# A DeltaNet layer whose decay comes from selecting products and a mask, whose triangular and attention matrices are written transposed, and whose projections and groups of heads run in another order

## The chip, the cores and the metric

One core of one Trainium2 chip runs the whole program. The metric is the device time of one execution in microseconds (us); smaller is better. The engines are TensorE (PE, its weight loads PEld), VectorE (DVE), ScalarE (ACT), GpSimd (POOL) and the queue of SyncE (SP), which issues nearly all DMAs. All data is float32; the program splits operands into a high and a low part and multiplies them in three products, so that the results keep float32 accuracy.

## The reference

256 tokens of width 1024 pass through two layers: a retention mixer and a gated DeltaNet mixer, each followed by a SwiGLU mixer of width 2816. The change is in DeltaNet alone:

```python
qkv = silu(causal_depthwise_conv(proj_qkv, conv_w))      # 8 q heads, 8 k heads, 16 v heads of 128
q, k = l2norm(q) * 128 ** -0.5, l2norm(k)                # each shared by two v heads
g = -exp(a_log) * softplus(a + dt_bias)                  # log decay per token and v head
gcum = cumsum(g)                                         # within a chunk
decay_mat = where(causal, exp(gcum[:, None] - gcum[None, :]), 0)
a_mat = where(strict, (k * beta) @ k.T * decay_mat, 0)
u, w = triangular_solve(a_mat + eye, [v * beta, k * beta * exp(gcum)])
attn = where(causal, q @ k.T * decay_mat, 0)
# per chunk, with the state S carried on:
v_new = u - w @ S
o = (q * exp(gcum)) @ S + attn @ v_new
S = S * exp(g_last) + (k * exp(g_last - gcum)).T @ v_new
o = rmsnorm(o) * silu(z);  out = o @ w_out
```

The kernel uses chunks of 128 tokens, so there are two (c = 0 and 1).

## The kernel before

**Weights.** Every weight matrix comes in slabs of 128x1024 numbers (`slab`, lines 124 to 137): a DMA from SP's queue into `raw`, a copy on ACT into `whi` (line 131), a subtraction on DVE into `wlo` (line 133), three buffers of each. A slab then feeds 12 matmuls of 512 columns (projections by token: z and the output) or 24 of 256 columns (projections by channel: k, q and v), all through `mm3`, lines 139 to 141. There are 260 slabs; 64 belong to DeltaNet: 16 for z, 8 for k, 8 for q, 16 for v and 16 for the output. q, k and v also pass a convolution of four taps: one on ACT (line 721) and three on DVE (line 724) for each block of 128 channels, and a SiLU on ACT.

**Order.** `gdn` lists jobs in the order z0, k, q, z1, v0, z2, v1, v2, v3, z3 (z and v in four groups of four heads), then the output projection. Beside the jobs run generators, one step after each slab: `gates` (decay), `sumsq_T` and `amat` (norms and the matrix A), `invert` (the inverse of I + A), `attn`, and `inner` for each group of four heads. A tile scheduler then orders each engine's instructions once and for all, when the program is built; at run time each engine works in order and waits for semaphores.

**Decay.** `gates` makes, for 8 sets of four heads, two tiles 128x512 (`gmh`, `gml`, line 691, on DVE and POOL), which line 714 multiplies by an upper triangle; ACT takes the exponential of 512 columns at a time (line 715). POOL sets what lies above the diagonal to zero (line 806).

**A and its inverse.** Line 768 makes k k.T, and A is that times beta and decay: on DVE for chunk 0 (line 778), on ACT and POOL for chunk 1 (lines 773, 774). The diagonal blocks of 32 go to DRAM and back in another layout (lines 797, 799); DVE inverts 128 of them side by side in 31 steps (lines 813, 815); the result goes through DRAM again (lines 820, 823: `Vd`, `Vc`). Then TensorE joins blocks to 64 (lines 849, 857, 864) and to 128 (lines 873, 882), chunk 0 before chunk 1, with an ACT copy after each step.

**Attention and heads.** Line 914 makes q k.T, ACT copies it, POOL multiplies it by the decay (`att`, line 917), TensorE transposes, ACT copies back into `D`. `inner` solves (line 938), moves the state (line 952), attends (line 946), takes norms (line 984, POOL's power in line 987), scales by z (line 995) and transposes for the output projection (`yh`, `yl`), which starts with group 0 and needs group 3 for its last quarter.

Of the kernel before, what the change touches and what calls it, by code (L numbers as in the profile page):

```python
# [61 lines left out]
class Trunk:  # L62
# [264 lines left out]
    def out_proj(self, w, yT, nk, nxt, early=None):  # L327
# [45 lines left out]
        p0 = self.proj_tok(w, 0, 512, yT, nk, None, (early,) if early else (), (), first)  # L373
        p1 = self.proj_tok(w, 512, 512, yT, nk, None, (early,) if early else (), (last,), second)
# [258 lines left out]
    def gates(self, b):  # L633
# [19 lines left out]
        nega, ax, e, u, ln, ru, g, gl = (tmp[:, i] for i in range(8))  # L653
# [26 lines left out]
        b["beta"] = beta  # L680

        slb = self.SL.unsqueeze(1).broadcast_to([P, 4, P])
        f4 = lambda x: x.rearrange("p h j -> p (h j)")
        b["D"] = [self.big(f"D{c}") for c in range(NT)]
        pend = []
        for c in range(NT):
            for hg in range(4):
                hs = slice(hg * 4, hg * 4 + 4)
                gm = [self.t2(n, dt=F32R) for n in ("gmh", "gml")]
                for eng, x, y in zip((V, V if hg % 2 else G), gm, (gh.bitcast(F32), gl)):  # L690
                    eng.tensor_tensor(x, slb, y[:, c, hs].unsqueeze(2).broadcast_to([P, 4, P]), ALU.mult)
                pend.append((c, hs, gm))
                if len(pend) == 3:
                    self.decay(b, Ur, *pend.pop(0))
                if hg % 2:
                    yield
                if c == 0 and hg == 1:

                    gs = self.psip()
                    for x in range(NT):  # L700
                        T.matmul(gs[:, x * NH:(x + 1) * NH], self.U, g[:, x], start=True, stop=True)
                    T.matmul(gs[:, 2 * NH:3 * NH], self.SL, g[:, 0], start=True, stop=True)
                    eg, dec = sm("eg"), sm("dec", (NH,))
                    A_.activation(eg.rearrange("p c h -> p (c h)"), gs[:, 0:2 * NH], AF.Exp)
                    A_.activation(dec, gs[:, 2 * NH:3 * NH], AF.Exp)
                    b["eg"], b["dec"] = eg, dec
        for x in pend:
            self.decay(b, Ur, *x)
        b["decayed"] = True

    def decay(self, b, Ur, c, hs, gm):
        dp = self.psip()
        for i, x in enumerate(gm):
            self.nc.tensor.matmul(dp, Ur, x.rearrange("p h j -> p (h j)"), start=i == 0, stop=i == 1)
        b["exp"] = self.nc.scalar.activation(b["D"][c][:, hs].rearrange("p h j -> p (h j)"), dp, AF.Exp).ins
# [30 lines left out]
    def amat(self, b, sl):  # L746


        nc = self.nc
        V, G, A_, T = nc.vector, nc.gpsimd, nc.scalar, nc.tensor  # L750
        yield
        ks, hs = slice(2 * sl, 2 * sl + 2), slice(4 * sl, 4 * sl + 4)
        rk = self.ph.tile([P, NT, 2], F32, name="rk", bufs=2)
        V.tensor_scalar(rk, b["kss"][:, :, ks], EPS, None, ALU.add)
        G.tensor_tensor(rk, rk, self.mhalf[:, 0:4].rearrange("p (t h) -> p t h", t=NT), ALU.pow)
        yield
        rkb = rk.unsqueeze(3).broadcast_to([P, NT, 2, 2])
        w2 = lambda x: x[:, :, hs].rearrange("p t (h w) -> p t h w", w=2)
        beta1, beta2 = b["beta1"], b["beta2"]
        V.tensor_tensor(w2(beta1), w2(b["beta"]), rkb, ALU.mult)  # L760
        V.tensor_tensor(w2(beta2), w2(beta1), rkb, ALU.mult)
        V.scalar_tensor_tensor(b["beg"][:, hs], beta2[:, 1, hs], -1.0, b["eg"][:, 1, hs], ALU.mult, ALU.mult)
# [20 lines left out]
    def invert(self, b):  # L783
# [19 lines left out]
        for c in range(NT):  # L803
            for hg in range(4):
                dm = b["D"][c][:, hg * 4:hg * 4 + 4]
                G.affine_select(dm, dm, [[0, 4], [-1, P]], ALU.is_ge, 0.0, base=0, channel_multiplier=1)
# [3 lines left out]
        for i in range(31):  # L810
# [3 lines left out]
                            Ab[:, n:32, i].unsqueeze(1).broadcast_to([P, n, m]), ALU.mult)  # L814
# [12 lines left out]
        yield  # L827
        yield
# [4 lines left out]
        V.transpose(Tc.rearrange("p a b -> p (a b)"), Vc.rearrange("p a b -> p (a b)"))  # L833
# [3 lines left out]
        for c in range(NT):  # L837
# [9 lines left out]
            for h in range(NH):  # L847
                for (q, b0, b1), x in zip(blocks, xp):
                    T.matmul(x[b0, h], Am[c][b1, h, b0], Vc[b1, c * NH + h], start=True, stop=True,
                             tile_position=(32 * q + 32, 32 * q))  # L850
            for (q, b0, b1), x in zip(blocks, xp):
                A_.copy(X[b0], x[b0])
            yield
            vp = [h32(self.psip()) for _ in blocks]
            for h in range(NH):
                for (q, b0, b1), x in zip(blocks, vp):
                    T.matmul(x[b0, h], Tc[b0, c * NH + h], X[b0, h], start=True, stop=True,
                             tile_position=(32 * q, 32 * q))
# [4 lines left out]
            for h in range(NH):  # L863
                T.matmul(tq[b1, h], X[b0, h], Tc[b0, c * NH + h], start=True, stop=True, tile_position=(0, 32))
# [4 lines left out]
            for hg in range(2):  # L869
                xp = h64(self.psip())  # L870
                for j in range(8):
                    h = hg * 8 + j
                    T.matmul(xp[lo, j], Am[c][up, h, lo], Vf[c][up, h, up], start=True, stop=True,
                             tile_position=(64, 0))
                X2.append(self.t2("X2", (8, 64), p=64))
                A_.copy(X2[hg], xp[lo])
            yield
            for hg in range(2):
                vp = h64(self.psip())
                for j in range(8):  # L880
                    h = hg * 8 + j
                    T.matmul(vp[lo, j], T2[lo, h], X2[hg][:, j], start=True, stop=True, tile_position=(0, 0))  # L882
# [4 lines left out]
    def attn(self, b):  # L887
# [13 lines left out]
        def flush(c, hp, at):  # L901
            tp = self.pstp().rearrange("p (x j) -> p x j", j=P)
            for j in range(4):
                self.transpose(tp[:, j], at[:, j])
            nc.scalar.copy(b["D"][c][:, 4 * hp:4 * hp + 4], tp)

        pend = None
        for c in range(NT):
            cs = slice(c * P, (c + 1) * P)
            for hp in range(4):  # L910
                at = self.t2("att")
# [283 lines left out]
```

## Time and profile before

| | us |
|---|---|
| median of 3 runs (873.5 to 874.11) | 873.65 |
| the profiled execution | 873.93 |
| its span, first to last instruction | 872.1 |
| DeltaNet in it, from its first weight-side matmul to the end of the output projection | 409.4 to 674.1 |

| in DeltaNet | us from the span's start |
|---|---|
| z0 | 409.4 to 419.7 |
| k, decay among it | 419.7 to 447.0 |
| q | 447.0 to 477.3 |
| z1 | 477.3 to 490.4 |
| v0, z2 | 490.4 to 524.7 |
| v1, v2, v3 | 524.7 to 577.4 |
| z3, the second chunk's inverse | 577.4 to 593.3 |
| the heads, no projection | 593.3 to 625.8 |
| output projection | 625.8 to 674.1 |

The page puts TensorE at 97% of the span, VectorE at 64%, ScalarE at 52% and GpSimd at 7%. The ends of matmuls are modelled, so what a matmul costs in a full stream is read from one start to the next. The granted clock is an average over a stretch of TensorE's two levels, 2.4 GHz (1.0) and 1.2 GHz (0.5).

### The profile page before, as it was taken

The numbers are of one execution on the slowest core, as the hardware profiler recorded it, in microseconds if no ns is written. First come the engines' busy times: TensorE is split into PE (matmuls) and PEld (weight loads), VectorE is DVE, ScalarE is ACT, GpSimd is POOL, SyncE is SP. The second block draws the span as 40 slices with busy tenths as digits, with TensorE's granted clock in tenths as the row PEclk, the third lists the DMA queues.
The fourth block names the chain that finished last, engine by engine and source line by source line (L and its number), as shares of the span: only waits on it lengthen the run. The fifth ranks groups of instructions, "written<-read, shape, count | busy, mean of one in ns | idle before, by whom it ended". The sixth has DMA issues, their size and how long they took to land.

```text
span 872.1 us, 12737 instructions
## 1 busy us (share of the span) xinstructions
PE 843.0 (97%) x4903; PEld 720.0 (83%) x4903; DVE 555.6 (64%) x828; ACT 453.0 (52%) x770; POOL 59.0 (7%) x59
## 2 busy tenths in 40 slices
PE   6999999999999999999999988999899999999996
PEld 5889987887788889886998878989788888889885
DVE  4957877655555555455889899854665555555453
ACT  5553235554544444344587745687845544444343
POOL 1000000000000000000217141000200000000000
PEclk9999999999999999999999999999999999999999
DMA  8666445455556555554555734732045656555551
GB/s 254 208 190 173 123 146 166 172 191 195 178 183 192 181 183 176 187 191 121 145 146 130 210 109 136 206 107 74 1 166 171 198 188 190 177 188 176 186 193 72
DMA packets 121806, 143.54 MB, mean 165 GB/s; under 512 B 14145, under 2 KB 67826, under 8 KB 121746
## 3 DMA queue, kind: packets, MB, share of 16 engines
q1 hardware_dynamic: 121234, 141.48, 51.7%
q0 software_dynamic: 368, 1.19, 0.5%
q8 instruction: 38, 0.62, 0.3%
q14 instruction: 22, 0.18, 0.1%
q10 hardware_dynamic: 144, 0.07, 0.0%
HBM read 140.62 MB, written 2.10 MB: 164 GB/s over the span
## 4 chain that ended last, share of the span: by engine, by line
PE 37%; DVE 8%; issue 2%; DMA 2%; ACT 2%; POOL 1%; SPq 0%; POOLq 0%; ACTq 0%; DVEq 0%
PE mm L140 10%; PE mm L141 10%; PE mm L139 10%; DVE wlo L133 2%; PE tp L200 1%; DVE cacc L724 1%; PE ip L952 1%; DVE pr L813 1%; DMA raw<-gdn_w_in 1%; PE ip L938 1%; PE ip L946 1%; DMA Vc<-Vd 1%; DMA Vd<-Vb 0%; DVE Vb L815 0%; PE ip L882 0%
## 5 line engine op out<-in xcount | busy, mean ns | idle before, releaser
L133 DVE TENSOR_TENSOR wlo<-raw,whi 128x1024 fp32r<-128x1024 f32 x260 | 321.0, 1235 | 231.5 <-ACT whi L131 229.5
L131 ACT CAST whi<-raw 128x1024 fp32r<-128x1024 f32 x260 | 273.4, 1052 | 300.3 <-PE mm L140 227.7
L139 PE MATMUL mm<-whi,xh 128*128 128x512 f32 (+1 forms) x576 | 220.5, 386 | 2.5 <-ACT whi L131 1.7
L140 PE MATMUL mm<-whi,xl 128*128 128x512 f32 (+1 forms) x576 | 219.8, 382 | 0.5 <-DVE xl L311 0.3
L141 PE MATMUL mm<-wlo,xh 128*128 128x512 f32 (+1 forms) x576 | 208.6, 383 | 1.2 <-DVE wlo L133 1.2
L139 PEld LDWEIGHTS mm<-whi,xh 128*128 128x128 f32 x576 | 109.3, 190 | 22.4 <-ACT whi L131 2.2
L141 PEld LDWEIGHTS mm<-wlo,xh 128*128 128x128 f32 x576 | 108.7, 189 | 21.9 <-DVE wlo L133 1.9
L140 PEld LDWEIGHTS mm<-whi,xl 128*128 128x128 f32 x576 | 109.0, 189 | 20.9 <-issue 0.7
L139 PE MATMUL mm<-xh,whi 128*128 128x256 f32 x384 | 111.9, 291 | 0.0
L140 PE MATMUL mm<-xh,wlo 128*128 128x256 f32 x384 | 110.2, 287 | 1.2 <-DVE wlo L133 1.2
L141 PE MATMUL mm<-xl,whi 128*128 128x256 f32 x384 | 109.8, 286 | 0.0
L140 PEld LDWEIGHTS mm<-xh,wlo 128*128 128x128 f32 x384 | 74.2, 193 | 3.3 <-DVE wlo L133 1.8
L139 PEld LDWEIGHTS mm<-xh,whi 128*128 128x128 f32 x384 | 74.1, 193 | 1.3 <-issue 0.5
L141 PEld LDWEIGHTS mm<-xl,whi 128*128 128x128 f32 x384 | 74.1, 193 | 0.3
L139 PE MATMUL mm<-whi,hh 128*128 128x512 f32 x176 | 69.8, 396 | 0.0
L140 PE MATMUL mm<-whi,hl 128*128 128x512 f32 x176 | 69.6, 396 | 0.0
L141 PE MATMUL mm<-wlo,hh 128*128 128x512 f32 x176 | 64.3, 396 | 0.0
L724 DVE SCALAR_TENSOR_TENSOR cacc<-mm,conv,cacc 128x253 f32<-128x253 f32 (+2 forms) x96 | 45.6, 511 | 9.0 <-ACT cacc L721 8.4
L140 PE MATMUL mm<-whi,yl 128*128 128x512 f32 x128 | 50.4, 394 | 0.0
L139 PE MATMUL mm<-whi,yh 128*128 128x512 f32 x128 | 49.5, 394 | 0.9 <-DVE v L995 0.9
L141 PE MATMUL mm<-wlo,yh 128*128 128x512 f32 x128 | 49.2, 396 | 0.0
L141 PEld LDWEIGHTS mm<-wlo,hh 128*128 128x128 f32 x176 | 33.1, 188 | 8.1
(235 smaller groups left out, 877.3 us busy)
## 6 DMA issues: line engine op xcount, KB each, us to landing
raw<-ffn_w_in SPq DMA_DIRECT2D x88, 512.0 KB, 3.5
raw<-ret_w_in SPq DMA_DIRECT2D x48, 512.0 KB, 3.9
raw<-gdn_w_in SPq DMA_DIRECT2D x48, 512.0 KB, 3.9
raw<-ffn_w_out SPq DMA_DIRECT2D x44, 512.0 KB, 3.5
raw<-ret_w_out SPq DMA_DIRECT2D x16, 512.0 KB, 3.2
raw<-gdn_w_out SPq DMA_DIRECT2D x16, 512.0 KB, 3.6
h<-x SPq DMA_DIRECT2D x4, 256.0 KB, 7.3
out<-o SPq DMA_DIRECT2D x4, 256.0 KB, 2.2
```

The lines of the kernel that those rows point to most:

```text
L131: nc.scalar.copy(hi, raw)
L133: lo_ = nc.vector.tensor_tensor(lo, raw, hi.bitcast(F32), ALU.subtract)
L139: t.matmul(out, lh, rh, start=first, stop=False)
L140: t.matmul(out, ll, rh, start=False, stop=False)
L141: self.last_mm = t.matmul(out, lh, rl, start=False, stop=last).ins
L200: self.nc.tensor.transpose(out, in_, self.ident[:n, :n])
L724: self.nc.vector.scalar_tensor_tensor(acc[:, s:S], ps[:, 0:S - s], cw[:, i, blk:blk + 1], acc[:, s:S], ALU.mult, ALU.add)
L813: V.tensor_tensor(tmp, Vb[:, 0:n, i:i + 1].broadcast_to([P, n, m]), Ab[:, n:32, i].unsqueeze(1).broadcast_to([P, n, m]), ALU.mult)
L938: T.matmul(up[:, j], b["V"][c][:, 4 * hg + j], v[c][:, j], start=True, stop=True)
L946: T.matmul(op[:, j], b["D"][c][:, 4 * hg + j], uu[:, j], start=True, stop=True)
L952: T.matmul(f4(op[:, 2 * j:2 * j + 2]), x(2 * hg + j), f4(st[:, 2 * j:2 * j + 2]), start=True, stop=True)
```

## The change

The decay is now a difference of running sums. One matmul with a triangle gives the sums of all heads as rows (`gcT`, four copies on the partitions, one for each 32 rows); for a set of four heads a first matmul adds -1e30 above the diagonal (`never`), and one matmul per head, with 32 rows of a stationary tile that selects one row of the sums (`tile_position=(32 * hg, 0)`), adds the sum of the column's token; the exponential then subtracts the row's own sum as a bias, one head of 128 columns at a time. The result is the transposed decay with the zeros in it. k k.T is symmetric and q k.T is made as k q.T, so A and attention come out transposed: DVE writes both straight from PSUM, and the transposes, copies and POOL's products and masks go. The joins of the inverse swap their operands. v is scaled by k's norm instead of beta times the inverse norm, and beta enters when a solve is read out (`uu`), now on DVE. The projections run z0, k, q, z1, z2, z3, v0 to v3. A group of heads starts when the group before has done two steps. The output projection goes through both column halves of one group of heads before the next.

```diff
-        gh = self.ph.tile([P, NT, NH], F32R, name="gh")
-        V.tensor_copy(gh, g)
-        V.tensor_tensor(gl, g, gh.bitcast(F32), ALU.subtract)
-        Ur = self.t1("Ur", (P,), F32R)
-        V.tensor_copy(Ur, self.U)
+        Uc = self.t1("Uc", (P,))
+        V.tensor_scalar(Uc, self.U, self.U[:, 63:64], None, ALU.subtract)
+        g4 = self.t1("g4", (4, NT * NH))
+        V.tensor_copy(g4, g.rearrange("p c h -> p (c h)").unsqueeze(1).broadcast_to([P, 4, NT * NH]))
+        gp = self.psip()
+        T.matmul(gp[:, 0:P], g4.rearrange("p r x -> p (r x)"), Uc, start=True, stop=True)
+        gcT = self.t1("gcT", (P,))
+        V.tensor_copy(gcT, gp[:, 0:P])
...
+        self.transpose(gs[:, 0:NT * NH], gcT[0:NT * NH])
...
+        V.tensor_scalar(negc, gs[:, 0:NT * NH], -1.0, None, ALU.mult)
...
+        V.tensor_scalar(never, self.SL, -1e30, None, ALU.mult)
+        V.tensor_copy(eye, self.ident)
         for c in range(NT):
+            dp = [self.psip().rearrange("p (h i) -> p h i", h=4) for _ in range(4)]
+            for x in dp:
+                T.matmul(x, eye, never.unsqueeze(1).broadcast_to([P, 4, P]), start=True, stop=False)
+            for j in range(4):
+                for hg in range(4):
+                    r = slice(32 * hg, 32 * hg + 32)
+                    n = 32 * hg + c * NH + 4 * hg + j
+                    T.matmul(dp[hg][:, j], self.ident[r, n:n + 1].broadcast_to([32, P]), gcT[r], start=False, stop=j == 3,
+                             tile_position=(32 * hg, 0))
+            yield
             for hg in range(4):
-                hs = slice(hg * 4, hg * 4 + 4)
-                gm = [self.t2(n, dt=F32R) for n in ("gmh", "gml")]
-                for eng, x, y in zip((V, V if hg % 2 else G), gm, (gh.bitcast(F32), gl)):
-                    eng.tensor_tensor(x, slb, y[:, c, hs].unsqueeze(2).broadcast_to([P, 4, P]), ALU.mult)
-                pend.append((c, hs, gm))
-                if len(pend) == 3:
-                    self.decay(b, Ur, *pend.pop(0))
+                for j in range(4):
+                    h = 4 * hg + j
+                    b["exp"] = A_.activation(b["D"][c][:, h], dp[hg][:, j], AF.Exp,
+                                             bias=negc[:, c * NH + h:c * NH + h + 1]).ins
...
-            if c >= 1:
-                kk = self.t2("kk")
-                for j in range(4):
-                    h = 4 * sl + j
-                    A_.activation(kk[:, j], pp[:, j // 2], AF.Copy, scale=beta2[:, c, h:h + 1])
-                G.tensor_tensor(b["A"][c][:, 4 * sl:4 * sl + 4], kk, b["D"][c][:, 4 * sl:4 * sl + 4], ALU.mult)
-                continue
...
-                G.affine_select(dm, dm, [[0, 4], [-1, P]], ALU.is_ge, 0.0, base=0, channel_multiplier=1)
...
-                    T.matmul(x[b0, h], Am[c][b1, h, b0], Vc[b1, c * NH + h], start=True, stop=True,
-                             tile_position=(32 * q + 32, 32 * q))
+                    T.matmul(x[b1, h], Am[c][b0, h, b1], Tc[b0, c * NH + h], start=True, stop=True,
+                             tile_position=(32 * q, 32 * q + 32))
...
-                    T.matmul(pp[:, j], b["qT"][:, 2 * hp + j, cs], b["kT"][:, 2 * hp + j, cs], start=True, stop=True)
-                kq = self.t2("kq", (2, P))
-                nc.scalar.copy(kq, pp[:, 0:2])
-                G.tensor_tensor(at.rearrange("p (j w) x -> p j w x", w=2),
...
-                    flush(*pend)
-                pend = (c, hp, at)
+                    T.matmul(pp[:, j], b["kT"][:, 2 * hp + j, cs], b["qT"][:, 2 * hp + j, cs], start=True, stop=True)
+                dv = b["D"][c][:, 4 * hp:4 * hp + 4].rearrange("p (j w) x -> p j w x", w=2)
+                V.tensor_tensor(dv, pp[:, 0:2].unsqueeze(2).broadcast_to([P, 2, 2, P]), dv, ALU.mult)
...
+        while not (b.get("inverted") and b.get("attended") and (hg == 0 or b["steps"].get(hg - 1, 0) >= 2)):
+            yield
...
-            A_.copy(f4(uu), f4(up))
+            V.tensor_tensor(uu, up, b["beta2"][:, c, hs].unsqueeze(2).broadcast_to([P, 4, P]), ALU.mult)
...
-                for j in range(2):
-                    h = 4 * hg + 2 * sl + j
-                    A_.activation(v[t][:, 2 * sl + j], tp[:, j, t], AF.Copy, scale=b["beta1"][:, t, h:h + 1])
+                h = 2 * hg + sl
+                A_.activation(v[t][:, 2 * sl:2 * sl + 2], tp[:, :, t], AF.Copy, scale=b["kn"][:, t, h:h + 1])
...
-        for group in "z0 k q z1 v0 z2 v1 v2 v3 z3".split():
+        for group in "z0 k q z1 z2 z3 v0 v1 v2 v3".split():
...
-        self.out_proj(w_out, yT, 16, nxt, early=6)
+        self.out_proj(w_out, yT, 16, nxt, early=(2, 4, 6))
```

TensorE's order in the first half of k, before, where `gmh` and `gml` (parts of the masked log decay) are multiplied by the triangle `Ur` among the projection's matmuls (`mm`):

```order
L141 MATMUL mm<-xl,whi 128x256
L714 MATMUL ip<-gmh,Ur 128x512
L139 MATMUL mm<-xh,whi 128x256
L140 MATMUL mm<-xh,wlo 128x256
L141 MATMUL mm<-xl,whi 128x256
L139 MATMUL mm<-xh,whi 128x256
L714 MATMUL ip<-gml,Ur 128x512
L140 MATMUL mm<-xh,wlo 128x256
```

and now, where the second chunk's decay stands (`never` the mask, `gcT` the running sums; each row of `gcT` is one head's selecting matmul, times the number at its end):

```order
L140 MATMUL mm<-xh,wlo 128x256
L705 MATMUL ip<-never,eye 128x512
L710 MATMUL ip<-gcT,cst 128x128 x4
L705 MATMUL ip<-never,eye 128x512
L710 MATMUL ip<-gcT,cst 128x128 x4
L705 MATMUL ip<-never,eye 128x512
L710 MATMUL ip<-gcT,cst 128x128 x4
L705 MATMUL ip<-never,eye 128x512
L710 MATMUL ip<-gcT,cst 128x128 x4
L141 MATMUL mm<-xl,whi 128x256
```

Sixteen products of 512 columns spread among the projections became eight, with 32 selecting matmuls behind them in two blocks; in the first chunk's block the four sets of heads take turns.

ScalarE's order in the same place, before (`D` is the decay, 512 columns each; `cacc` a convolution's first tap):

```order
L131 CAST whi<-raw 128x1024
L715 ACTIVATE D_3517<-ip 128x512 x3
L131 CAST whi<-raw 128x1024
L715 ACTIVATE D_3517<-ip 128x512
L721 ACTIVATE cacc<-mm,conv 128x256 x2
L715 ACTIVATE D_3518<-ip 128x512
L131 CAST whi<-raw 128x1024
L715 ACTIVATE D_3518<-ip 128x512 x2
L131 CAST whi<-raw 128x1024
L715 ACTIVATE D_3518<-ip 128x512
L1039 ACT_TABLE_LOAD
```

and now (`negc` is the bias, 128 columns each; `kT` and `zs` wait for the other table):

```order
L716 ACTIVATE D_3550<-ip,negc 128x128 x16
L726 ACTIVATE cacc<-mm,conv 128x256
L131 CAST whi<-raw 128x1024
L716 ACTIVATE D_3551<-ip,negc 128x128 x12
L726 ACTIVATE cacc<-mm,conv 128x256
L716 ACTIVATE D_3551<-ip,negc 128x128 x4
L1024 ACT_TABLE_LOAD
L1024 ACTIVATE zs_3412<-zs_3412 128x512
L1050 ACTIVATE kT<-cacc 128x256 x3
L1024 ACTIVATE zs_3412<-zs_3412 128x512
L131 CAST whi<-raw 128x1024
```

Between the two chunks' exponentials there is one weight copy where there were four; the next follows only after the table load and five SiLUs.

TensorE's order near the end of the projections, before (joins of the inverse to 128, in chunk 0, then the first join of chunk 1, with the projection of v on both sides; `Vc` and `T` hold inverse blocks, `X` the middle product, `vc` is v to be transposed):

```order
L139 MATMUL mm<-xh,whi 128x256
L882 MATMUL ip<-X_5243,T_5056 64x64 x8
L882 MATMUL ip<-X_5254,T_5056 64x64 x8
L200 MATMUL tp<-cst,vc 128x128 x4
L849 MATMUL ip<-Vc,A_3420 32x32 x32
L140 MATMUL mm<-xh,wlo 128x256
L141 MATMUL mm<-xl,whi 128x256
```

and now, from the last projecting matmul on:

```order
L141 MATMUL mm<-xl,whi 128x256
L852 MATMUL ip<-Vc,X 32x32 x32
L859 MATMUL tp<-X,Vc 32x32 x16
L200 MATMUL tp<-cst,vc 128x128 x4
L868 MATMUL ip<-T_4988,A_3418 64x64 x16
L877 MATMUL ip<-Vf_4815,X_5174 64x64 x8
L877 MATMUL ip<-Vf_4815,X_5185 64x64 x8
L200 MATMUL tp<-cst,vc 128x128 x4
L844 MATMUL ip<-Tc,A_3419 32x32 x32
L852 MATMUL ip<-Vc,X 32x32 x32
L859 MATMUL tp<-X,Vc 32x32 x16
```

All projections of v and z now stand ahead of the joins, of which only the first (line 844, chunk 0) stands among them, ten projecting matmuls before the row shown first.

## Rows read from the trace of the kernel before

**Rows 1.** Stages: length, busy PE, PEld, DVE, ACT, POOL; clock, DMA share, GB/s.
```profile
419.70:447.00 27.30, 27.30 (x215) 26.59 (x215) 24.91 (x46) 18.18 (x34) 5.75 (x4) 1.00 0.56 154
477.30:490.40 13.10, 11.93 (x56) 9.49 (x55) 10.33 (x17) 8.83 (x27) 2.84 (x3) 1.00 0.84 217
490.40:524.70 34.30, 31.75 (x209) 28.82 (x208) 33.44 (x60) 20.31 (x48) 13.05 (x8) 0.95 0.47 133
524.70:577.40 52.70, 49.31 (x597) 47.14 (x596) 43.37 (x80) 33.30 (x63) 2.60 (x2) 0.97 0.57 160
577.40:593.30 15.90, 15.90 (x182) 13.01 (x180) 9.79 (x15) 11.21 (x22) 0.00 (x0) 1.00 0.37 115
593.30:625.80 32.50, 29.57 (x214) 27.37 (x213) 15.22 (x45) 27.75 (x94) 3.27 (x2) 0.95 0.07 26
625.80:674.10 48.30, 48.26 (x227) 39.32 (x228) 30.54 (x51) 24.78 (x49) 3.27 (x2) 1.00 0.45 148
sum 264.70, PE 254.12 PEld 229.00 DVE 201.64 ACT 174.93 POOL 47.69; mean PE 28.24 PEld 25.44 DVE 22.40 ACT 19.44 POOL 5.30
```
**Rows 2.** TensorE in order of time, two places: start, us, instruction, count.
```profile
574.88 1.54 PE L849 MATMUL ip<-Vc,A 32*32 32x32 f32 x64
576.35 0.39 PE L140 MATMUL mm<-xh,wlo 128*128 128x256 f32 x1
...
577.28 0.28 PE L141 MATMUL mm<-xl,whi 128*128 128x256 f32 x1
577.40 0.40 PE L139 MATMUL mm<-whi,xh 128*128 128x512 f32 x1
577.64 0.40 PE L140 MATMUL mm<-whi,xl 128*128 128x512 f32 x1
...
589.26 1.90 PE L873 MATMUL ip<-Vf,A 64*64 64x64 f32 x29
```
**Rows 3.** The same view, at the heads: state, attention, state, attention.
```profile
599.44 1.05 PE L946 MATMUL ip<-uu,D 128*128 128x128 f32 x8
600.33 1.03 PE L952 MATMUL ip<-du,kn 128*128 128x256 f32 x4
601.20 1.05 PE L946 MATMUL ip<-uu,D 128*128 128x128 f32 x8
```
**Rows 4.** VectorE and GpSimd in order of time, a group's norm and scaling.
```profile
613.73 0.69 DVE L977 TENSOR_TENSOR v<-ip,qs 128x512 f32<-128x512 f32 x1 [3.80 <-ACT uu L940]
...
616.64 1.64 POOL L987 TENSOR_TENSOR f<-f,mhalf 128x8 f32<-128x8 f32 x1 [86.36 <-DVE f L986]
...
618.51 2.19 DVE L995 SCALAR_TENSOR_TENSOR v<-v,f,zs 128x128 f32<-128x128 f32 x8
```
**Rows 5.** Groups of ScalarE's instructions in DeltaNet: busy, mean ns; idle before, releaser.
```profile
L131 ACT CAST whi<-raw 128x1024 fp32r<-128x1024 f32 x63 | 66.1, 1051 | 37.0 <-PE mm L140 22.8 <-DMA raw<-gdn_w_in 10.1 <-PE mm L141 3.9
L721 ACT ACTIVATE cacc<-mm,conv 128x256 f32<-128x256 f32 x32 | 14.8, 469 | 4.2 <-PE mm L141 3.1 <-DVE cacc L724 1.0
L715 ACT ACTIVATE D<-ip 128x512 f32<-128x512 f32 x8 | 4.8, 598 | 1.7 <-PE ip L714 1.7
L973 ACT ACTIVATE qs<-ip,eg 128x128 f32<-128x128 f32 x16 | 4.7, 382 | 1.0 <-PE ip L952 0.8
L1039 ACT ACT_TABLE_LOAD x1 | 1.3, 1283 | 0.0
```
**Rows 6.** ScalarE in order of time: four scaled copies of 128 columns, two of 512.
```profile
605.54 1.11 ACT L1047 ACTIVATE zs<-mm 128x512 f32<-128x512 f32 x2
606.50 1.19 ACT L973 ACTIVATE qs<-ip,eg 128x128 f32<-128x128 f32 x4
```
**Rows 7.** The chain that ended last, in time: start, us, what.
```profile
465.72 2.45 DVE rk L754
```
**Rows 8.** DMA issues by line: KB each, median us to landing.
```profile
Vd<-Vb SPq DMA_DIRECT2D x1, 512.0 KB, 4.2
Vc<-Vd SPq DMA_DIRECT2D x1, 512.0 KB, 4.5
```

More of the change, by code (lines that the diff above doesn't have):

```diff
@@ L325, in sumsq1, with out_proj @@
                                   accum_out=self.ss[:, i, t:t + 1])
-    def out_proj(self, w, yT, nk, nxt, early=None):
+    def out_proj(self, w, yT, nk, nxt, early=()):
         kind, l = nxt
@@ L372, in out_proj @@
         last = -(-nk // 2) - 2
-        p0 = self.proj_tok(w, 0, 512, yT, nk, None, (early,) if early else (), (), first)
-        p1 = self.proj_tok(w, 512, 512, yT, nk, None, (early,) if early else (), (last,), second)
+        p0 = self.proj_tok(w, 0, 512, yT, nk, None, early, (), first)
+        p1 = self.proj_tok(w, 512, 512, yT, nk, None, early, (last,), second)
         for x in zip(p0, p1):
@@ L652, in gates @@
         tmp = self.t1("tmp", (8, NT, NH))
-        nega, ax, e, u, ln, ru, g, gl = (tmp[:, i] for i in range(8))
+        nega, ax, e, u, ln, ru, g = (tmp[:, i] for i in range(7))
         beta = sm("beta")
@@ L680, in gates @@
         b["beta"] = beta
-        slb = self.SL.unsqueeze(1).broadcast_to([P, 4, P])
-        f4 = lambda x: x.rearrange("p h j -> p (h j)")
+        yield
+        gs = self.psip()
+        self.transpose(gs[:, 0:NT * NH], gcT[0:NT * NH])
+        for x in range(NT):
+            T.matmul(gs[:, 64 + x * NH:64 + (x + 1) * NH], self.U, g[:, x], start=True, stop=True)
+        T.matmul(gs[:, 64 + 2 * NH:64 + 3 * NH], self.SL, g[:, 0], start=True, stop=True)
+        negc, eg, dec, nege = sm("negc", (NT * NH,)), sm("eg"), sm("dec", (NH,)), sm("nege", (NH,))
@@ L695, in gates @@
                 if hg % 2:
                     yield
[L697 to L706, printed above, removed]
@@ L707, in gates @@
-        for x in pend:
-            self.decay(b, Ur, *x)
-        b["decayed"] = True
[L711 to L715, printed above, removed]
+        b["decayed"] = True
     def taps(self, ps, blk):
@@ L826, in invert @@
             G.memset(Vf[c], 0.0)
-        yield
-        yield
+        for _ in range(4):
+            yield
+        V.transpose(Tc.rearrange("p a b -> p (a b)"), Vc.rearrange("p a b -> p (a b)"))
         for c in range(NT):
@@ L856, in invert @@
                 for (q, b0, b1), x in zip(blocks, vp):
-                    T.matmul(x[b0, h], Tc[b0, c * NH + h], X[b0, h], start=True, stop=True,
-                             tile_position=(32 * q, 32 * q))
+                    T.matmul(x[b0, h], X[b1, h], Vc[b1, c * NH + h], start=True, stop=True,
+                             tile_position=(32 * q + 32, 32 * q))
             for (q, b0, b1), x in zip(blocks, vp):
@@ L863, in invert @@
             for h in range(NH):
-                T.matmul(tq[b1, h], X[b0, h], Tc[b0, c * NH + h], start=True, stop=True, tile_position=(0, 32))
+                T.matmul(tq[b1, h], Vc[b1, c * NH + h], X[b1, h], start=True, stop=True, tile_position=(32, 32))
             A_.activation(T2[b1, :, 0:32], tq[b1], AF.Copy, scale=-1.0)
@@ L872, in invert @@
                     h = hg * 8 + j
[L873 to L876, printed above, removed]
+                    T.matmul(xp[up, j], Am[c][lo, h, up], T2[lo, h], start=True, stop=True,
+                             tile_position=(0, 64))
+                X2.append(self.t2("X2", (8, 64))[up])
+                A_.copy(X2[hg], xp[up])
             yield
@@ L881, in invert @@
                     h = hg * 8 + j
-                    T.matmul(vp[lo, j], T2[lo, h], X2[hg][:, j], start=True, stop=True, tile_position=(0, 0))
+                    T.matmul(vp[lo, j], X2[hg][:, j], Vf[c][up, h, up], start=True, stop=True, tile_position=(64, 0))
                 A_.activation(Vf[c][lo, hg * 8:hg * 8 + 8, up], vp[lo], AF.Copy, scale=-1.0)
@@ L899, in attn @@
         V.tensor_tensor(b["cc"].rearrange("p t (h w) -> p t h w", w=2), rqb, rqb, ALU.mult)
[L901 to L907, printed above, removed]
         for c in range(NT):
@@ L953, in by_state @@
             return op
-        yield
-        while not (b.get("inverted") and b.get("attended")):
-            yield
         u0 = solve(0)
@@ L1011, in gdn @@
         w_in, w_out = a["gdn_w_in"][0], a["gdn_w_out"][0]
-        b = {"y": [], "z": set()}
+        b = {"y": [], "z": set(), "steps": {}}
         self.open("gdn")
@@ L1021, in begin @@
             b["zs"] = [self.g4(f"zs{hg}", (NT, 4, P)) for hg in range(4)]
[L1022 to L1024 removed]
+            b["beta2"] = self.ph.tile([P, NT, 16], F32, name="beta2")
+            b["kn"] = self.ph.tile([P, NT, 8], F32, name="kn")
             b["A"] = [self.big(f"A{c}") for c in range(NT)]
```

44 lines of the change are left out of this document (21 added, 23 removed).

## The prediction, made before the changed kernel ran

> **What bounds the kernel now.** I read the stages first (the busy time of each engine from one stretch to the next), then TensorE in order of time, to get what a matmul costs from one start to the next, then ScalarE's groups, and last the chain of waits. In DeltaNet's 264.7 us TensorE is busy for 254.1 [rows 1], so its own queue sets the time, and a change is worth what it takes from that queue or from its waits. The waits that show are 1.2, 2.6 and 3.4 us in three stages of the projections and 2.9 where the heads run without a projection. In the second of these VectorE is busy for 33.4 of 34.3 us and GpSimd for 13.1. The granted clock is 0.95, 0.97 and 0.95 in three stages, which at the lower level of 1.2 GHz (0.5) is about 3.4 us in each [rows 1].
>
> The prices, from start to start: a matmul of 256 columns 0.12 us, of 512 columns 0.24 [rows 2]; at the heads each float32 matmul stands twice in the trace, and eight such records of 128 columns take 0.89, 0.11 each, four of 256 columns 0.87 [rows 3]. The joins of the inverse take 1.47 us for 64 records of 32x32, 0.023 each, and about 2.0 for 32 records of 64x64 [rows 2].
>
> **The change on TensorE's path, up to the last matmul of a projection that is not the output's.** Before, that point lies 183.9 us after 409.4, at 593.3.
>
> *Joins that move behind it.* A chunk's joins are two of 64 records (1.47 each), one of 32 records (about 0.9, between half and all of the former), two of 64x64 (2.0 each): 7.8 us [rows 2]. Before, all but the last 2.0 of both chunks lie ahead of the point, 13.7; now only the first join, 1.5. Of eight sets of transposes of v five lay ahead, now one: 4 sets of four at 0.11, 1.8. Together -14.0, which comes back below.
>
> *Decay.* Sixteen products of 512 columns go, eight come: -8 x 0.24 = -1.9. The 32 selecting matmuls are 64 records of 128 columns. In the second chunk four stand in a row at one position: 32 x 0.11 = 3.5. In the first the sets take turns, and I take half, 1.8. With 0.4 for the new sums: +3.8. Bounds: all 64 at the 0.023 of the small joins [rows 2] gives 0, all at 0.11 gives +5.5. The small joins take turns between two positions, which is why I don't take 0.11 for all. The Trainium skill (TensorEngine Tiling (Array Packing), Key Properties) says that "different tiles can execute LdWeights and Matmul in parallel"; if four at once held for the first chunk, the sum would be 1 us lower. The same list says that a change of tiling mode drains the engine, which speaks against the eight alternations here; where the trace leaves the 32x32 joins for a 128x128 matmul, at 576.35, no gap shows [rows 2].
>
> *Attention.* 32 transposes at 0.11 go: -3.5. Its products with the decay move from GpSimd to VectorE, eight of 512 columns from PSUM, by the nearest row 0.7 each [rows 4].
>
> *ScalarE among the decay.* Eight exponentials of 512 columns (0.6 each [rows 5]) become 32 of 128 with a bias. None is shown; the nearest are scaled copies of 128 columns from PSUM, four in 1.19 us [rows 6], 0.29 each, so 16 take 4.7. After the first 16 come a first tap and one weight copy, 6.1 in all; after the next 16 a tap, a table load of 1.3, two SiLUs of 512 columns (0.56 each [rows 6]), three of 256 (0.37), and only then the weight copy for k's eighth slab (1.05): 9.6 more, and 1.2 on VectorE, 16.9 in all [rows 5, 6]. When the first exponentials start, 93 of k's matmuls have been issued by the order, 3.9 slabs of 24, and TensorE has 3.1 slabs of 24 x 0.12 and the second chunk's decay (4 x 0.24 + 3.5) to do before it needs the eighth: 13.4. It waits for the weights: +3.5, and I take +3. Bounds: at a quarter of a 512-column exponential, 0.15, the wait is gone; at 0.38 [rows 5] it is 6.
>
> *Waits that go.* The attention products (most of GpSimd's 13.1 us in v0 and z2), the masks and half of A leave GpSimd, and ScalarE loses copies. VectorE gains 16 products of A (0.27, by the scalings of the same size), eight of attention and eight `uu` (0.7), and loses twelve of `gmh` and `gml` (0.7 as well): 15.5 against 8.4 [rows 4]. That is 7 us more, spread over 184, in which it was busy for 201.6 - 15.2 - 30.5 = 155.9 [rows 1]. Beside it, z1 to z3 in one piece leave it over half of each slab's time for the 31 steps of the inverse, where before these lay beside taps of v. One of its instructions, of four numbers a partition, lasted 2.45 us beside GpSimd's power [rows 7]. The Trainium skill (SBUF — State Buffer, SBUF: two separate sides) calls the port pair that the two engines share "an exclusive lock, not a bandwidth split"; by that rule all of GpSimd's time that goes, not some, would be VectorE's again, which is the first rival's case. Of 7.1 us of waits and up to 3.3 lost at the low clock I take half: -5; bounds -10 and 0.
>
> The point then lies at 183.9 - 14.0 + 3.8 - 3.5 + 3 - 5 = 168.2 us, at 577.6.
>
> **From there to the output projection.** Before, 32.5 us: the heads alone, three groups at once. Now the joins stand here with nothing to fill their waits, and each needs ScalarE, whose queue also holds the rest of v: one weight copy (1.0), 20 copies of 512 columns (0.56), 22 of 256 (SiLUs, scalings, first taps, 0.37 by the tap's 0.47 less the overlap of 0.1): 20.3, of which 1.1 lies before the point. First solve at +19.2. To the first state product 4.1: solve 0.9, a tap of the last block ahead of `uu` in VectorE's queue 1.2, `uu` and `du` 0.7 each, handovers. From there TensorE's order has 14 products of 0.87 to 0.89 and two sets of transposes before group 0's second attention is done: 13.3 [rows 3]. Then the sum 0.7, norm, GpSimd 1.6, eight scalings 2.2 (7.0 from 613.73 to 620.7 before [rows 4]), transposes 0.9, copy 0.7: 9. Together 45.6, and 1.2 for a stretch at 1.2 GHz beyond the one that was here: 46.8, so +14.3. Bounds: 40, if taps and joins run side by side, and 53.
>
> **The output projection** took 48.3 us with two products of group 3 among it (1.8). Now it holds six (5.3): +3.5. Its waits were 0.04 [rows 1], and I see no new one: y1 follows y0 by less than the four slabs (11 us) on y0.
>
> **Sum.** -14.0 + 3.8 - 3.5 + 3 - 5 + 14.3 + 3.5 = +2.1 us. The profiled execution took 873.93, 0.3 above the median of the runs; added to that median, with 0.4 for the handovers that I have set at 0.1 to 0.2, I forecast 876.2.
>
> **Rivals.**
>
> *VectorE was the real bound before the point (faster).* For it: VectorE's 33.4 of 34.3 us, GpSimd's stalls, and that the inverse's steps now lie beside z1 to z3, which have no taps. Then all 10 us of waits go (-5 more), the selecting matmuls cost 1.5 (-3.8), and the weight copies among the exponentials come in time (-3): 11.8 off the sum, 864. I take 866, since not all three need come whole. Against it: TensorE's waits there are only 7.1 us, the joins stand after the projections in TensorE's order however early the inverse is, and the exponentials lie in one block. It decides if the first output matmul comes before 617.
>
> *The inverse comes late (much slower).* The steps on VectorE end about two slabs before the last projection; the way through DRAM is 4.2 + 4.5 us [rows 8], and the first join stands ten matmuls before the end. There is no slack: each microsecond by which the last step comes later than 11 us before the point moves all that follows. With 6 us of it and a longer stretch at the low clock, 884.
>
> *The parts cancel (no change).* Each of my terms is a few us and they differ in sign; with the stall among the exponentials at 1 and the tail at 45, the sum is within 0.2%, 873 to 875. A measurement of this kernel can hardly tell 0.2%, 1.7 us, from no change.
>
> **How the numbers follow.** Forecast (876.2, its own range 873 to 881) 0.46; VectorE the bound 0.30; late inverse 0.12; cancelling 0.12. Of the forecast 0.08 lies within 0.2% and 0.03 below; that makes slower 0.47, same 0.20, faster 0.33. The range 866 to 884 reaches to the middle of the faster and of the late case and leaves out a fifth.
>
> **What would show it.** In the changed trace: a wait of TensorE for `wlo` or `whi` of some 3 us after the exponentials, with 16 of them in 4.7 us; the last v matmul near 578 and the first output matmul near 624, with ScalarE nearly full from one to the first solve; TensorE busy for less than 38 of those 46 us; GpSimd at far less than its 47.7 us in DeltaNet [rows 1], and attention's products on VectorE at 0.7 each. I am wrong if TensorE waits for nothing in k, if the joins run while projections are left, or if the output projection ends before 670.

## The result and the profile after

The changed kernel takes 877.18 us (median of 12 runs, 876.02 to 884.41), the kernel before 873.43 beside it: a ratio of 1.0051, 95% interval 1.0035 to 1.0068. It is slower by half a per cent, 1 us from the forecast. The profiled execution took 876.53, 2.6 more than that of before; DeltaNet, from 409.4 to the end of the output projection, took 267.1 instead of 264.7 [rows 1].

The stages of the changed kernel: length, busy PE, PEld, DVE, ACT, POOL, then clock, DMA share, GB/s. The first goes to the last projection matmul, the second and third are the joins, the fourth the heads, the fifth the output projection.

```profile
409.40:571.10 161.70, 160.31 (x1213) 149.06 (x1213) 127.35 (x274) 98.89 (x222) 11.40 (x7) 0.99 0.60 165
571.10:583.55 12.45, 9.85 (x242) 9.10 (x242) 8.52 (x16) 11.26 (x23) 0.00 (x0) 1.00 0.26 88
583.55:597.20 13.65, 13.65 (x171) 13.14 (x168) 4.89 (x11) 8.84 (x20) 0.00 (x0) 0.51 0.01 2
597.20:624.68 27.48, 23.35 (x156) 21.81 (x155) 15.66 (x42) 18.02 (x69) 2.60 (x2) 0.94 0.01 1
624.68:676.54 51.86, 51.86 (x248) 42.82 (x249) 34.70 (x63) 27.55 (x58) 3.95 (x3) 1.00 0.43 139
sum 267.14, PE 259.02 PEld 235.93 DVE 191.12 ACT 164.55 POOL 17.94; mean PE 51.80 PEld 47.19 DVE 38.22 ACT 32.91 POOL 3.59
```

The point that the prediction puts at 577.6 comes at 571.1, 22.2 us earlier than before. The 32.5 us from it to the output projection have become 53.6, and the output projection takes 51.9 instead of 48.3: -22.2 + 21.1 + 3.6 = +2.5.

The same 2.5 can be read in another way. The loss at the low clock is length x (1 - clock), summed over the rows: 9.9 us after (1.6 + 6.7 + 1.6), 4.9 before [rows 1]. TensorE's busy time without it is 259.0 - 9.9 = 249.1 after and 254.1 - 4.9 = 249.2 before: the change leaves TensorE the same work. Its idle time falls from 10.6 to 8.1 and the clock's loss doubles. On this sum, an estimate since a slow matmul isn't always waited for, the change would have gained 2.5 us at the clock of before. The twelve executions of the changed kernel point the same way: the eight of 876.0 to 877.4 us had a mean clock of 0.984 to 0.986 over the whole span, those of 878.1 and 879.1 us 0.980 and 0.982, those of 881.3 and 884.4 us 0.976 and 0.973. That shows that clock and time go together, not by itself which leads.

TensorE in order of time shows where the clock went (start, us, instruction, count). The two chunks' joins are the same work:

```profile
571.12 1.70 PE L852 MATMUL ip<-Vc,X 32*32 32x32 f32 x61
574.83 2.08 PE L868 MATMUL ip<-T,A 64*64 64x64 f32 x32 [0.41 <-ACT T L860]
577.18 2.04 PE L877 MATMUL ip<-Vf,X 64*64 64x64 f32 x32 [0.28 <-ACT X L871]
...
583.25 2.67 PE L852 MATMUL ip<-Vc,X 32*32 32x32 f32 x61 [1.91 <-ACT X L847]
588.57 3.35 PE L868 MATMUL ip<-T,A 64*64 64x64 f32 x29
591.99 3.30 PE L877 MATMUL ip<-Vf,X 64*64 64x64 f32 x29
```

The first chunk runs at 2.4 GHz, the second at 1.2. From the second join (L852) to the start of the transposes behind the last join, the first chunk takes 8.0 us (571.1 to 579.15), the second 12.0 (583.25 to 595.22).

And the decay, PE and ACT in order of time:

```profile
432.86 1.16 PE L710 MATMUL ip<-gcT,cst 32*128 32x128 f32 x22
434.38 1.15 PE L710 MATMUL ip<-gcT,cst 32*128 32x128 f32 x10
...
437.60 0.40 PE L705 MATMUL ip<-never,eye 128*128 128x512 f32 x1
437.92 1.15 PE L710 MATMUL ip<-gcT,cst 32*128 32x128 f32 x8
439.01 0.51 PE L705 MATMUL ip<-never,eye 128*128 128x512 f32 x1
439.44 1.15 PE L710 MATMUL ip<-gcT,cst 32*128 32x128 f32 x8
...
443.99 0.42 PE L140 MATMUL mm<-xh,wlo 128*128 128x256 f32 x1
444.20 0.42 PE L141 MATMUL mm<-xl,whi 128*128 128x256 f32 x1
...
447.30 0.28 PE L141 MATMUL mm<-xl,whi 128*128 128x256 f32 x1
447.42 0.28 PE L139 MATMUL mm<-xh,whi 128*128 128x256 f32 x1
```
```profile
434.05 4.23 ACT L716 ACTIVATE D<-ip,negc 128x128 f32<-128x128 f32 x16 [1.37 <-PE ip L710]
```

Behind the selecting matmuls k's products stand 0.21 us apart until 447.0, and 0.12 from there: 3.4 us at 1.2 GHz, not a wait for weights. In a row at one position eight selecting records take 1.09 us to the next start (437.92 to 439.01), where eight full-size ones take 0.89 [rows 3], and the mask between two sets 0.43 (439.01 to 439.44).

### The profile page after: what moved, and what is told of

Its sections match the earlier page's. It is cut to its first block, busy times and chain, and to the rows that moved or that the text cites. A ratio compares the mean times of both kernels' runs of the same rounds, so it can differ in the third digit from the quotient of the medians.

```text
span 874.5 us, 12764 instructions
## 1 busy us (share of the span) xinstructions
PE 847.7 (97%) x4930; PEld 726.8 (83%) x4930; DVE 545.1 (62%) x852; ACT 442.3 (51%) x738; POOL 29.2 (3%) x35
## 4 chain that ended last, share of the span: by engine, by line
PE 48%; ACT 3%; DVE 1%; issue 1%; POOLq 0%; POOL 0%; ACTq 0%; DVEq 0%
PE mm L141 13%; PE mm L139 13%; PE mm L140 13%; PE tp L200 2%; PE ip L941 1%; PE ip L710 1%; PE ip L935 1%; ACT junk L970 1%; PE ip L852 1%; PE ip L927 0%; ACT v L1083 0%; DVE cacc L729 0%; PE ip L901 0%; PE ip L774 0%; PE ip L868 0%
```

## The experiments

Each stands beside runs of the kernel before on the same chip; ratios are to these. "Low" is time at 1.2 GHz between 409 and 677 in the profiled execution (before 10.2 us, after 20.5). A profiled execution isn't always near its run's median: with the order of before and with 2 and 3 steps a slab it took 3.6, 3.0 and 4.1 us less, in the runs of 867.04 and 871.53 us 3.0 and 2.7 more.

**The order alone.** The kernel before with one line changed:

```
-        for group in "z0 k q z1 v0 z2 v1 v2 v3 z3".split():
+        for group in "z0 k q z1 z2 z3 v0 v1 v2 v3".split():
```

> The kernel before with only the order of the units changed (z1, z2, z3 ahead of v0 to v3). Theory A (in the changed kernel 20 us of joins stand behind the last projection, uncovered, and cost 6.8 us there at 1.2 GHz and 3.8 us of waits more; the order itself is harmless): here the joins stay among the projections and the first heads too, so 867 to 872 us, faster than before. Theory B (the new order leaves v3's taps and copies, 20 us of ScalarE, beside the joins and heads, and that is the loss): 876 to 880, slower than before.

873.38 us, ratio 1.0000 (0.9989 to 1.0011). Neither theory. The inverse's last step comes at 538.3 instead of 546.8, the first output matmul at 616.7 instead of 625.8, and the low time is 6.8; but the output projection holds more of the heads' work and takes 56.9 (before 48.3), and TensorE waits for VectorE where taps, steps and `wlo` meet. Waits of TensorE (us in total, times, longest):

```profile
PE mm L141 <- DVE wlo L133: 3.8, 3, 1.4
PE mm L140 <- DVE wlo L133: 2.2, 2, 1.9
```

So the order is not what made the changed kernel slower.

**The order of before in the changed kernel.** The same line, the other way.

> The changed kernel with the order of the units of before (z3 last). Theory A: every join now stands behind the last projection, none among it, so the time is that of the changed kernel, 875 to 879, with 571 to 596 again at a mean clock below 0.85. Theory B: no v work is left on ScalarE there, the joins' waits go, 868 to 872.

884.15 us, ratio 1.0121 (1.0095 to 1.0146), more than either theory has. TensorE's joins and the first heads stand wholly behind z3, and low time is 34.1 us. The stage of it, columns as above:

```profile
575.80:606.50 30.70, 29.53 (x383) 27.75 (x379) 7.55 (x13) 17.64 (x35) 0.00 (x0) 0.50 0.10 36
```

ScalarE is free for 13 of these 30.7 us, so its queue isn't the limit; theory B falls.

**More steps a slab.** `b["pace"] = 1` becomes 2, and 3.

> The changed kernel with twice as many steps of the inverse a slab, so that the joins of the first chunk and part of the second stand among the last 85 projection matmuls. Theory A: about half of the 10.6 us come back, 870 to 873, and the granted clock is 1.0 beside the joins that stand among projections. Theory B (the joins wait for ScalarE wherever they stand, and VectorE is full at 61 of 69 us): 876 to 880.

> The changed kernel with three times as many steps a slab: all joins and the first half of the heads stand among projections. Theory A: nearly all of the 10.6 us come back, 864 to 870. Theory B: the steps hold up the weights' wlo on VectorE (3 us of steps and 1.2 of wlo against a slab of 2.9), TensorE waits 5 to 10 us for them, 876 to 885.

881.46 us, ratio 1.0090 (1.0071 to 1.0109), and 891.32, 1.0196 (1.0170 to 1.0221). Theory A's cure fails. With 2, low time falls to 13.7 but TensorE idles 11.8 (after 8.1); with 3 its queue has the first join ahead of projections, while VectorE isn't done, and low time is 29.5, most of it from inside that wait on:

```profile
PE mm L139 <- DVE cacc L729: 4.3, 2, 3.2
```
```profile
PE ip L844 <- DVE Tc L824: 17.1, 1, 17.1
```

The first is with 2 steps, the second with 3. Forcing the inverse ahead on a VectorE that has the changed kernel's work brings waits in place of the loss, and with 3 steps more time at the low level too.

**The old decay.** In the changed kernel the decay goes back to 16 products of 512 columns with `gmh` and `gml`, 8 exponentials and the masks on GpSimd, for the transposed form:

```
-        never, eye = self.t1("never", (P,), F32R), self.t1("eye", (P,), F32R)
...
+        ub = self.U.unsqueeze(1).broadcast_to([P, 4, P])
...
+                    eng.tensor_tensor(x, ub, y[:, c, hs].unsqueeze(2).broadcast_to([P, 4, P]), ALU.mult)
...
+                    self.decay(b, Lr, *pend.pop(0))
...
+                G.affine_select(dm, dm, [[0, 4], [1, P]], ALU.is_ge, 0.0, base=0, channel_multiplier=-1)
```

> The changed kernel with the decay made as before (products of g with a triangle on VectorE and GpSimd, 16 products of 512 columns, 8 exponentials, masks on GpSimd), now for the transposed form; all else as changed. Theory C (TensorE's own work, at full clock, is the same before and after, since the selecting products cost 6.1 us more than what they replace and the transposes that go give 4 back; what is left is waits and the low clock): 6.1 us of work go and the stretch at 1.2 GHz behind the decay (443 to 447, 1.6 us), 868 to 871. Theory D (VectorE and ScalarE set the pace, so that work taken from TensorE in k becomes a wait, the more so as gmh, gml and the masks come back): 875 to 879.

874.88 us, ratio 1.0018 (1.0005 to 1.0030): 2.3 less than the changed kernel, not 6 to 9. The last projection matmul comes 9.2 us earlier (561.7), so theory C's work is gone from TensorE; what it gave is lost behind that point, where TensorE is at the low level from 2 us after the first join (562.8) to deep in the heads:

```profile
409.40:564.80 155.40, 152.40 (x1155) 142.85 (x1154) 137.15 (x285) 95.81 (x200) 24.10 (x19) 1.00 0.63 176
564.80:602.30 37.50, 34.88 (x422) 32.77 (x423) 14.55 (x29) 21.01 (x44) 0.00 (x0) 0.50 0.05 17
```

**Filler behind the joins.**

```
+        def warm(m):
+            wp = self.psip()
+            with self.tc.issue_after(m.ins):
+                for _ in range(4):
+                    T.matmul(wp[:, 0:S], xh[:, 0:P], xh, start=True, stop=True)
...
+            warm(m)
```

> The changed kernel with four products of 128x256 that nobody reads behind each group of joins (48 in all, 48 x 0.12 = 5.8 us of TensorE). Theory C: the granted clock stays at or near 1.0 from 571 to 597, the joins take 1.5 to 2.0 us a set again in both chunks (6.8 us less), the filler lies partly in the waits of 2.6 us, and the first output matmul comes at 620 to 624: 872 to 876. Theory D: the joins wait for ScalarE's copies whatever the clock, and the filler adds up: first output matmul 628 to 631, 880 to 883.

> The old decay and the filler together. Theory C: both gains add, 864 to 869. Theory D: 878 to 884.

884.51 us, ratio 1.0129 (1.0108 to 1.0151); with the old decay 888.87, 1.0177 (1.0156 to 1.0198). The filler doesn't hold the clock. In the first of the two TensorE was busy by its records for 15.6 us before it fell:

```profile
570.40:586.00 15.60, 15.60 (x317) 14.23 (x316) 7.50 (x14) 11.92 (x24) 0.00 (x0) 1.00 0.23 70
586.00:610.00 24.00, 22.14 (x156) 19.98 (x154) 8.09 (x17) 9.81 (x21) 0.00 (x0) 0.50 0.01 2
```

```profile
574.14 1.14 PE L878 MATMUL ip<-T,A 64*64 64x64 f32 x16
575.21 0.74 PE L838 MATMUL ip<-xh 128*128 128x256 f32 x4
575.88 1.14 PE L878 MATMUL ip<-T,A 64*64 64x64 f32 x16
```

So the clock falls here without a wait, and full-size products among small tiles, 0.67 us behind each 1.07 here, didn't prevent it. That waits play no part elsewhere isn't shown: in the changed kernel the fall (583.7) comes right behind the wait of 1.91 us for `X`. The time is about that of theory D, but not for D's reason: TensorE waits for no copy at these joins. Theory C's cure fails; its account of the time is not refuted by this, nor proved.

**Selecting matmuls in turns.** Each selecting matmul is issued behind the last one of the set before it in program order, so that both chunks go round the four positions:

```
+                    with self.tc.issue_after(nv):
+                        nv = T.matmul(dp[hg][:, j], self.ident[r, n:n + 1].broadcast_to([32, P]), gcT[r], ...
```

> The changed kernel with the selecting matmuls of both chunks forced to take turns among the four 32-row positions. If turns are what made 22 records of the first chunk 0.05 us each against 0.11 to 0.14 where four stand in a row: 42 records x 0.07 = 3 us less in the decay, though the exponentials, and with them the inverse, start two slabs later; 873 to 877. If the price doesn't hang on turns: the decay keeps its 9.4 us, 877 to 882.

884.12 us, ratio 1.0124 (1.0102 to 1.0145). The price follows the turns, more than I had expected; the time does not:

```profile
435.12 1.17 PE L711 MATMUL ip<-gcT,cst 32*128 32x128 f32 x32
441.39 1.17 PE L711 MATMUL ip<-gcT,cst 32*128 32x128 f32 x32
```

32 records in 1.17 us, where eight at one position took 1.15. Behind these two blocks the clock doesn't fall; the stage up to the last projection matmul:

```profile
409.40:565.40 156.00, 152.31 (x1147) 142.44 (x1146) 123.76 (x269) 95.07 (x217) 11.40 (x7) 1.00 0.60 168
```

But the exponentials come later (436.5 instead of 434.0), TensorE waits 4.0 us for `Tc`, and 41 us from 570.4 on run at the low level.

**GpSimd's products again.** Attention's products and those of A's second chunk go back to GpSimd, with ScalarE's copies:

```
-                V.tensor_tensor(dv, pp[:, 0:2].unsqueeze(2).broadcast_to([P, 2, 2, P]), dv, ALU.mult)
+                kq = self.t2("kq", (2, P))
+                self.nc.scalar.copy(kq, pp[:, 0:2])
+                G.tensor_tensor(dv, kq.unsqueeze(2).broadcast_to([P, 2, 2, P]), dv, ALU.mult)
...
+            if c >= 1:
...
+                    A_.activation(kk[:, j], pp[:, j // 2], AF.Copy, scale=beta2[:, c, h:h + 1])
+                G.tensor_tensor(b["A"][c][:, 4 * sl:4 * sl + 4], kk, b["D"][c][:, 4 * sl:4 * sl + 4], ALU.mult)
```

> The changed kernel with attention's products and half of A's on GpSimd again (copies by ScalarE, as before), the transposed form and the selecting decay kept. Theory E (VectorE's products among the steps are what brings the inverse late; joins that stand alone put TensorE at 1.2 GHz, here they have 13 to 32 projection products between the sets): less than 10 us at 1.2 GHz from 409 to 680 instead of 20.5, first output matmul 616 to 620, 869 to 874. Theory F (VectorE, with wlo and the taps, holds TensorE up as soon as the joins stand among projections, as the waits of 12 us did with two steps a slab): low clock down, waits up by as much, 876 to 881.

870.31 us, ratio 0.9970 (0.9958 to 0.9981): theory E, and 6.9 us less than the changed kernel. The steps of the inverse in the changed kernel and in this one (times, duration in ns, first and last start):

```profile
L808 DVE TENSOR_TENSOR pr<-Vb,Ab x31: 193/359/425, 496.8 to 556.4; 128x31 f32<-128x31 f32 x2, 128x60 f32<-128x60 f32 x2, 128x87 f32<-128x87 f32 x2, 128x112 f32<-128x112 f32 x2
```
```profile
L815 DVE TENSOR_TENSOR pr<-Vb,Ab x31: 191/374/1315, 492.6 to 542.9; 128x31 f32<-128x31 f32 x2, 128x60 f32<-128x60 f32 x2, 128x87 f32<-128x87 f32 x2, 128x112 f32<-128x112 f32 x2
```

A step lasts longer beside GpSimd (up to 1.3 us against 0.4), and yet the last comes 13.5 us sooner. The joins then stand among v's projections and the clock holds; its low time, 6.8 us, lies at the second chunk's selecting matmuls and behind them (442.0 to 448.9). DeltaNet takes 259.9 us instead of 267.1, with 13.7 us less at the low level and 5.4 us of idle time instead of 8.1. The stages of the joins and of the heads:

```profile
570.00:596.50 26.50, 25.40 (x361) 24.09 (x359) 14.82 (x26) 18.71 (x36) 0.00 (x0) 1.00 0.25 81
596.50:617.44 20.94, 18.91 (x138) 17.48 (x137) 15.35 (x43) 17.45 (x69) 2.54 (x2) 1.00 0.07 26
```

What this doesn't part is whether the products delay the steps by their own time or by the place that the program's order gives the steps among them, nor what attention's products do from what A's do.

**The old decay as well, and denser steps.**

> As the run with GpSimd's products, and the decay as before too: of the change there remain the transposed form (no transposes of attention, 32 x 0.12 = 3.8 us less of TensorE than before), the order and the staggered groups. Theory E: 866 to 871, faster than before. Theory F: 873 to 877.

> As the last, with steps of the inverse packed 1.7 times as densely, so that every set of joins has 17 or more projection products behind it. Theory E: no low stretch beside the joins, 863 to 869. Theory F: the denser steps hold up wlo on VectorE, 873 to 880.

867.04 us, ratio 0.9938 (0.9920 to 0.9956), and with `b["pace"] = 1.7` 871.53, 0.9984 (0.9971 to 0.9997). The first is as theory E has it; the second lies between the two, and denser steps again bring waits (TensorE: 3.9 us for `cacc`, 3.9 for `wlo`). The joins' stage of the first:

```profile
570.00:597.60 27.60, 25.40 (x360) 23.96 (x359) 14.93 (x27) 19.06 (x38) 0.00 (x0) 0.94 0.22 75
```

**No stagger.** ` and (hg == 0 or b["steps"].get(hg - 1, 0) >= 2)` is taken out of the kernel of 867.04.

> The fastest kernel so far (GpSimd's products and the old decay, 867.0 us) without the condition that a group of heads starts two steps behind the one ahead of it. If the stagger is worth something: group 0 shares TensorE and VectorE with group 1 again, the first output matmul comes 2 to 4 us later with the same work behind it, 869 to 872. If not: the groups' steps only change places, TensorE's work is the same, 866 to 868.

866.06 us, ratio 0.9926 (0.9910 to 0.9942), which overlaps with the other's interval: the stagger is worth nothing that these runs can tell. This is the fastest version. From the change it keeps the transposed form, the new order, (2, 4, 6), and the new places of k's norm and beta (v's scaling, `uu` on VectorE); decay, the other products and the start of the groups are as before. No run parts these four, so which of them gives the gain over the kernel before isn't shown; the order without the others gave none.

## Why the prediction came out as it did

The total was right, the kernel is slower, and the mechanism of the loss (joins moved behind the last projection, with nothing beside them) is the one forecast. But two steps were off by about the same, in opposite directions (-6.5 and +6.8 us), so that the total came out within 1 us is luck.

*Up to the last projection matmul: forecast 168.2 us, measured 161.7.* Joins and transposes of v: TensorE's records of them, summed from start to start, go from 15.4 to 1.4 us, -14.0 as forecast. Attention's transposes: -3.8 (-3.5). Decay: 3.5 + 5.9 us in place of 16 x 0.24, with 0.4 for the sums +6.0, above my +3.8 and its bound of 5.5. Within a row at one position the price was the forecast 0.11. What the sum lacks is the change between full-size and 32-row matmuls: eight records take 1.09 instead of 0.89, and the mask between two sets 0.43, where with turns a mask that stands among projections took 0.23:

```profile
439.08 0.39 PE L705 MATMUL ip<-never,eye 128*128 128x512 f32 x1
439.31 0.28 PE L141 MATMUL mm<-xl,whi 128*128 128x256 f32 x1
```

That is about 0.4 us there and back, six times in the two chunks, an estimate of 2.4 for a miss of 2.2. Full-size float32 records among projections have no such step: in the changed kernel four of them and the product behind take 0.56, which is 4 x 0.11 + 0.12:

```profile
468.07 0.60 PE L774 MATMUL ip<-kT 128*128 128x128 f32 x4
468.43 0.36 PE L141 MATMUL mm<-xl,whi 128*128 128x256 f32 x1
468.63 0.28 PE L139 MATMUL mm<-xh,whi 128*128 128x256 f32 x1
```

The stall among the exponentials: forecast 3, none. ScalarE's side came as forecast, with 16 exponentials in 4.23 us (4.7) and `wlo` of k's eighth slab ready 16.3 us after the first of them (16.9). TensorE needed it later, after 18.6 us instead of 13.4: the rest of the first chunk's decay, which the sum leaves out, took 1.4, the second chunk's decay 1.5 more than forecast, the low clock 1.7 and transposes of k 0.6. What I had named as the sign that I'm wrong, no wait in k, is there. Waits that go: 7.6 us of idle time became 1.4 (-6.2) and one of two low stretches went (-1.7), -7.9 against my -5. All of these give -19.7; the other 2.5 us are spread over the 942 projection matmuls and the transposes of q and k, and I can't assign them. One of the reasons for the term of -5 was misread: the VectorE instruction of 2.45 us [rows 7] lay beside GpSimd's memsets of `Vf` (464.59 to 468.15), not beside its power, which waits for it and starts at 468.26.

*From there to the output projection: forecast 46.8, measured 53.6, past my bound of 53.* The step that failed is "1.2 for a stretch at 1.2 GHz". The clock's loss here is 6.7 + 1.6 = 8.3 us, where I had 1.2 on top of the 1.6 of before: 5.5 of the 6.8 us. I took ScalarE as the limit of the joins, with the first solve 19.2 us behind the point; it came after 25.0, and ScalarE was busy for 20.1 of the 26.1 us from 571.1 to 597.2, and TensorE for 23.5, more than half of it at half speed. So "TensorE busy for less than 38 of 46 us" was wrong too: 46.9 of 53.6.

*The output projection: forecast 51.8, measured 51.9.* Attention's products on VectorE took 0.68 each (0.7), and GpSimd's time in DeltaNet fell from 47.7 to 17.9:

```profile
L903 DVE TENSOR_TENSOR D<-ip,D 128x512 f32<-128x512 f32 x8 | 5.3, 680 | 0.0
```

*The rivals.* "VectorE was the real bound" had it right that waits were to be had, but the first output matmul came at 624.7, not before 617. Its converse holds for the inverse: taking products off VectorE again made the kernel 6.9 us faster. "The inverse comes late" didn't come in as that rival has it: the last step (556.4) is 9.6 us later than before's 546.8, but 14.7 us ahead of the point, more than the 11 that it asks for. In the run with turns the step came at 558.4 and the projections ended at 565.4, 7.0 us apart; the time was 884.12, near the rival's 884, with 13.0 us idle and 41 at the low level. What the runs add is that neither the order in the kernel before (1.0000) nor the stagger brings anything by itself, and that the selecting decay and the products moved to VectorE take back what the rest of the change gives.

The Trainium skill (TensorEngine Tiling (Array Packing), Key Properties) says that tiles at different positions work in parallel. I had kept this out of the sum. The run with turns agrees with it: 32 records in 1.17 us against 8 in 1.15 at one position. The same list of the Trainium skill says that a change of tiling mode drains the engine. The traces agree: no idle time shows, but starts lie further apart, by the 0.4 us there and back above. My sum has no term for this, because no gap shows at 576.35 [rows 2]; there too the next product starts 0.22 us later, not 0.12:

```profile
576.35 0.39 PE L140 MATMUL mm<-xh,wlo 128*128 128x256 f32 x1
576.57 0.28 PE L141 MATMUL mm<-xl,whi 128*128 128x256 f32 x1
```

## What to carry to other kernels

Ask of a chain that is moved out from under other work not only what it waits for but at which clock it will run: here 26 us of small tiles by themselves cost more by the clock than by their waits. Before moving products to an engine because it saves a copy and a transpose, look at which serial chain shares that engine's queue and what stands behind the end of the chain. And test each part of a change alone: this one was half a per cent slower in whole, 0.7% faster than before without its decay, its products of A and attention on VectorE and its stagger.

## What the runs showed of the hardware

- Where the joins (tiles of 32x32 and 64x64) stood behind the last projection, 1.2 GHz followed in each run: in one piece 13.7 us in the changed kernel, 30.7 with the order of before, 37.5 with the old decay, 41.0 with turns and, with filler among them, 24.0. In the last TensorE had been busy by its records for 15.6 us without a wait; in the others waits stood ahead of the fall, the longest of 1.9, 1.7, 0.9 and 4.0 us. With projection matmuls between the sets the clock was 1.00 and 0.94 over the same joins.
- After 16 selecting matmuls of 32 rows in the second chunk (32 records, four matmuls in a row at each position), full-size products were 0.21 apart for 3.4 us, then 0.12. With turns they were 0.12 apart from the second on.
- A change between full-size and 32-row matmuls and back: about 0.4 us, from starts (1.09 for eight records instead of 0.89, 0.43 for the mask instead of 0.23).
- Float32 records of 128 columns at four positions of 32 rows in turn: 0.03 us each; at one position 0.11 within the row, 0.14 with the changes at its ends.
